# A list schedule with other prices: the same four-layer kernel, planned with instruction durations as costs

## The chip, the cores and the metric

One core of a Trainium2 chip runs the whole program in one launch. The metric is the time of one execution on the device in microseconds. The engines are TensorE (PE; its weight loads are listed as PEld), VectorE (DVE), ScalarE (ACT), GpSimd (POOL) and SyncE (SP), which issues most transfers.

## The reference

A model of four layers on 512 positions of width 1024, in fp32. Each layer is a mixer and a SwiGLU feed-forward part (FFN), each with an RMS norm ahead of it and added to the running sum `h`. The mixers are, in this order, RWKV-7, windowed attention with sinks, a gated spatial unit (SGU) and gated linear attention (GLA).

```python
h = x
for i in range(4):
    hn = rmsnorm(h, norm_mix[i])
    m = [rwkv7_mix, swa_sink_mix, sgu_chunk_mix, gla_mix][i](hn, ...)
    h = h + m
    h = h + swiglu(rmsnorm(h, norm_ffn[i]), ffn_w_in[i], ffn_w_out[i])
return rmsnorm(h, norm_final)

def swiglu(x, w_in, w_out):                  # 1024 -> 2 x 2816 -> 1024
    gate, up = jnp.split(x @ w_in, 2, axis=-1)
    return (jax.nn.silu(gate) * up) @ w_out

# within rwkv7_mix, for 16 heads of 64:
def step(state, inp):
    r_t, d_t, k_t, v_t, kk_t, a_t = inp
    sa = jnp.einsum('bhvk,bhk->bhv', state, kk_t)
    state = (state * d_t[:, :, None, :] - sa[..., None] * (kk_t * a_t)[:, :, None, :]
             + v_t[..., None] * k_t[:, :, None, :])
    return state, jnp.einsum('bhvk,bhk->bhv', state, r_t)
```

## The kernel before, in words

**Products.** A large fp32 product is made of three products in the type fp32r: weights and activations are each split into a high and a low part (`hi` by ScalarE, `lo = raw - hi` by VectorE), and `mm3` adds hi x hi, hi x lo and lo x hi in PSUM. The weights come in tiles of 128 x 1024 (`wraw`, eight buffers), and go through `whi` and `wlo` (four buffers each). The FFN uses a seven-product scheme over quarters (`seven`): each weight quarter is loaded by SP, and combinations of quarters are made by accumulating transfers that POOL issues. For a block of 512 hidden columns a `hidden` pass makes gate and up, and an `out_fast` pass multiplies the result by the output weights and adds into `h`. There are three such output parts in each FFN, fed by two hidden passes each. In an output part of full width there are 14 weight tiles, 16 additions into `h`, 8 combinations of activations and 14 splits of them.

**RWKV.** The scan is worked in chunks of 64 positions. The 16 heads are four groups of four. For each group `rwkv_prepare`, `rwkv_products` and `rwkv_inverse` make decays, scores and an inverse of a triangular matrix (together `ahead(n)`), and `rwkv_chain` goes through eight chunks one after the other: products with the state, a copy by ScalarE (`wu`), 64x64 products with the inverse (`iv`), a copy (`vu`), the state's update by VectorE (`st`), and the outputs. In program order `ahead(n + 1)` stands before the chain of group n. Score blocks are tiles `pa` and `pr`.

**The order.** The kernel isn't emitted as it is written. Every call on an engine is recorded (line 233 of the profile's kernel is the one place that calls the engines, so nearly all instructions bear L233) as an operation with a price: the time for which it occupies its engine, and a latency until its result can be used by a consumer. `Program.run` is a greedy list schedule over all operations. At each step it finds, for every engine, when the operations whose inputs are planned could start; it prefers the lowest in program order among those within `SLACK` (60 ns) of the earliest, in a window of 700 operations, takes the engine whose candidate starts first, and emits it. An operation that touches a tile not held yet also needs a free buffer of its kind, and for PSUM some more conditions. The result is a fixed order of instructions for each engine; on the chip each engine runs its own list in order and waits on semaphores.

**Prices.** `price` gives (occupancy, latency) in ns. `n` is the number of elements a partition, `columns` the number of per-partition scalar operands. An operation's result is ready at occupancy plus latency; the next one on the same engine, if it depends on nothing late, starts after the occupancy. A transposition has 109 ns, an fp32r product 0.4167 ns a column plus 13.5, an fp32 product 1.667 ns a column plus 5.

**Unused products.** The planner also keeps account of the columns that TensorE works on in each stretch of 3413 ns. Where the plan has TensorE waiting and the account is low, `keep_warm` puts in products of the identity with itself whose result nobody reads (line 453, tile `ident`). Their number comes out of the plan. In a stretch that follows one with too little work the plan doubles the cost of products.

Of the kernel before, what the change touches and what calls it, by code (L numbers as in the profile page):

```python
# [189 lines left out]
class Program:  # L190
# [71 lines left out]
    def price(self, eng, what, args, kw):  # L262

        views = [a for a in list(args) + list(kw.values()) if isinstance(a, View)]
        n = max(v.free() for v in views)
        columns = sum(v.free() == 1 and v is not views[0] and n > 1 for v in views)
        if what == "dma_start":
            return (490.0 if eng == "SP" else 1000.0), 2000.0
        if eng == "PE":
            if what == "transpose":  # L270
                return 109.0, 200.0
            m, n = args[1].free(), args[2].free()
            if args[2].dtype == F32R:
                return max(n * 0.4167 + 13.5, m * 0.83), 200.0
            return max(n * 1.667 + 5.0, m * 1.667, 340.0 if n < 16 and m == P else 0.0), 200.0
        if eng == "DVE":
            if what == "memset":
                return n * 1.05, 130.0
            fast = what in ("tensor_copy", "tensor_scalar") and not any(v.buf.psum for v in views)
            return 68.0 + n * (0.52 if fast else 1.042) + 61.0 * columns, 130.0  # L280
        if eng == "ACT":
            return (50.0 if any(v.buf.psum for v in views[1:]) else 92.0) + n * 0.833 + 94.0 * columns, 150.0
        if what == "tensor_copy":
            return 36.0 + n * 3.66, 130.0
        return 37.0 + n * (0.83 if len(views) < 3 else 2.8 if views[0].dims[-1][0] < 32 else 2.32), 130.0

    def run(self):
        ops, n = self.ops, len(self.ops)
# [1492 lines left out]
```

## Time and profile before

| | |
|---|---|
| median of 3 runs | 2627.5 us (2625.31 to 2631.97) |
| the profiled execution | 2641.05 us, its span 2639.3 us |
| mean granted TensorE clock | 0.982 |
| instructions | 34990 |
| busy: PE, PEld, DVE, ACT, POOL | 2554.7, 2083.4, 1853.8, 1331.6, 466.0 us |
| read from HBM | 359.51 MB |

The profile names an instruction by line, engine, operation and tiles (out<-in, buffer numbers left out). "Busy" is the union of the durations on an engine; durations of neighbours can overlap. "Idle before" is the engine's idle time ahead of the instructions of a group, and the arrow names what ended most of it. The windows give busy time in a stretch, the timeline single instructions in order of time, with those of one kind merged (x4 means four).

### The profile page before, as it was taken

How to read it: one execution, taken by the hardware profiler on the slowest of the kernel's cores; microseconds unless marked ns; L12 is line 12 of the kernel's file. 1: busy time of each engine (PE TensorE's matmuls, PEld its weight loads, DVE VectorE, ACT ScalarE, POOL GpSimd, SP SyncE). 2: the span in 40 equal slices, each digit the busy share in tenths (PEclk: the TensorE clock that was granted, in tenths of full speed). 3: DMA queues.
4: the chain of work that ended last, by engine and by line, in shares of the span. 5: the costliest groups of instructions: out<-in, count | busy, mean ns of one | idle time of the engine just before them, and what ended most of it. 6: DMA issues, size and time to landing. Idle time of an engine off the chain costs nothing.

```text
span 2639.3 us, 34990 instructions
## 1 busy us (share of the span) xinstructions
PE 2554.7 (97%) x12974; PEld 2083.4 (79%) x12974; DVE 1853.8 (70%) x2888; ACT 1331.6 (50%) x2208; POOL 466.0 (18%) x492
## 2 busy tenths in 40 slices
PE   8999889999999999999999999999999999999998
PEld 7667767889888775888787888898878777888886
DVE  8675777568787966676868474478777735577868
ACT  3544343356555655655555342365645633555545
POOL 1013333311212234121112000012121000012111
PEclk8989989999999999999999999999999999999999
DMA  3220001148988622499896222379897321389885
GB/s 126 72 68 9 7 7 37 39 126 219 226 215 213 178 84 50 101 223 229 208 227 185 96 96 88 80 176 224 211 228 170 119 96 50 81 221 223 209 209 125
DMA packets 127146, 366.24 MB, mean 139 GB/s; under 512 B 13424, under 2 KB 20976, under 8 KB 126976
## 3 DMA queue, kind: packets, MB, share of 16 engines
q0 software_dynamic: 41472, 138.43, 29.1%
q1 hardware_dynamic: 85504, 225.59, 25.3%
q8 instruction: 102, 1.67, 0.3%
q14 instruction: 68, 0.56, 0.1%
HBM read 359.51 MB, written 2.10 MB: 137 GB/s over the span
## 4 chain that ended last, share of the span: by engine, by line
PE 47%; DMA 5%; issue 5%; DVE 5%; ACT 2%; POOL 0%; SPq 0%; ACTq 0%; POOLq 0%; DVEq 0%
PE ps L233 47%; DMA wraw<-ffn_o_a 2%; DMA wraw<-ffn_w_b 2%; DVE slot L233 2%; DVE wlo L233 1%; ACT whi L233 1%; DVE left L233 1%; DMA wraw<-ffn_w_a 1%; ACT slot L233 1%; POOL wraw L233 0%; DVE h L233 0%; DVE mx L233 0%; DMA wraw<-ffn_o_b 0%; DMA slot<-sg_b_s 0%; DMA slot<-slot 0%
## 5 line engine op out<-in xcount | busy, mean ns | idle before, releaser
L233 PE MATMUL ps<-whi,slot 128*128 128x512 f32 (+1 forms) x5072 | 1548.3, 383 | 14.1 <-DVE slot L233 10.0
L233 PEld LDWEIGHTS ps<-whi,slot 128*128 128x128 f32 x5072 | 942.3, 188 | 190.2 <-issue 22.7
L233 DVE TENSOR_TENSOR wlo<-wraw,whi 128x1024 fp32r<-128x1024 f32 (+2 forms) x628 | 723.1, 1157 | 421.7 <-ACT whi L233 420.5
L233 ACT CAST whi<-wraw 128x1024 fp32r<-128x1024 f32 (+3 forms) x632 | 626.6, 995 | 695.5 <-PE ps L233 528.5
L233 PE MATMUL ps<-wlo,slot 128*128 128x512 f32 (+1 forms) x2536 | 969.3, 382 | 3.7 <-DVE wlo L233 3.6
L233 PEld LDWEIGHTS ps<-wlo,slot 128*128 128x128 f32 x2536 | 476.6, 188 | 87.4 <-DVE wlo L233 7.5
L233 PE MATMUL ps<-slot,whi 128*128 128x512 f32 (+2 forms) x864 | 275.0, 396 | 1.2 <-ACT slot L233 0.9
L233 POOL DMA_DIRECT2D wraw<-ffn_w_a x128 | 109.5, 857 | 502.7 <-DVE wlo L233 363.0
L233 DVE TENSOR_TENSOR slot<-ps,slot 128x512 f32<-128x512 f32 (+2 forms) x287 | 153.3, 566 | 60.4 <-PE ps L233 45.7
L233 PEld LDWEIGHTS ps<-slot,whi 128*128 128x128 f32 (+2 forms) x864 | 156.7, 184 | 48.6 <-issue 9.1
L233 POOL DMA_DIRECT2D wraw<-ffn_w_b x64 | 54.8, 864 | 744.6 <-DMA wraw<-ffn_w_b 505.8
L233 PE MATMUL ps<-slot,wlo 128*128 128x512 f32 (+2 forms) x432 | 169.7, 393 | 0.3 <-DVE wlo L233 0.3
L233 DVE TENSOR_TENSOR slot<-left,slot 128x512 fp32r<-128x512 f32 (+1 forms) x214 | 138.9, 666 | 34.9 <-ACT slot L233 29.1
L233 DVE TENSOR_TENSOR h<-h,ps 128x512 f32<-128x512 f32 x192 | 126.7, 682 | 26.4 <-PE ps L233 25.9
L233 ACT CAST slot<-left 128x512 fp32r<-128x512 f32 (+1 forms) x214 | 124.1, 606 | 31.8 <-PE ps L233 24.7
L233 POOL DMA_DIRECT2D wraw<-ffn_o_a x64 | 54.7, 854 | 278.4 <-DVE wlo L233 162.5
L233 ACT COPY slot<-ps 128x512 f32<-128x512 f32 (+2 forms) x137 | 76.1, 568 | 52.1 <-PE ps L233 51.8
L233 PEld LDWEIGHTS ps<-slot,wlo 128*128 128x128 f32 (+2 forms) x432 | 79.5, 184 | 21.2 <-DVE wlo L233 2.2
L233 PEld LDWEIGHTS ps<-ident,slot 128*128 128x128 f32 x580 | 68.3, 142 | 34.5 <-issue 9.5
L233 PE MATMUL ps<-ident,slot 128*128 128x128 f32 x580 | 89.6, 277 | 3.3 <-POOL slot L233 2.6
L233 ACT COPY left<-ps 128x512 f32<-128x512 f32 x100 | 50.6, 556 | 63.7 <-PE ps L233 63.7
L233 DVE TENSOR_TENSOR slot<-slot 128x512 fp32r<-128x512 f32 (+9 forms) x93 | 61.5, 666 | 18.5 <-ACT slot L233 17.1
(260 smaller groups left out, 2517.3 us busy)
## 6 DMA issues: line engine op xcount, KB each, us to landing
wraw<-ffn_w_a SPq DMA_DIRECT2D x128, 512.0 KB, 6.6
wraw<-ffn_w_a POOLq DMA_DIRECT2D x128, 512.0 KB, 6.0
wraw<-ffn_o_a SPq DMA_DIRECT2D x64, 512.0 KB, 4.8
wraw<-ffn_o_a POOLq DMA_DIRECT2D x64, 512.0 KB, 7.5
wraw<-ffn_w_b SPq DMA_DIRECT2D x64, 384.0 KB, 3.5
wraw<-ffn_w_b POOLq DMA_DIRECT2D x64, 384.0 KB, 6.5
wraw<-ffn_o_b SPq DMA_DIRECT2D x16, 512.0 KB, 5.5
wraw<-ffn_o_b POOLq DMA_DIRECT2D x16, 512.0 KB, 6.1
```

The costliest lines, as they stand in the source:

```text
L233: op = self.add(eng.name, lambda: getattr(eng.target, what)(*map(real, args), **{k: real(a) for k, a in kw.items()}), *self.price(eng.name ...
```

## The change

Only `price` is changed. For VectorE the fixed part goes from 68 to 148 ns and the latency from 130 to 60; a scan has 2.1 ns an element in place of 1.042. For ScalarE the fixed part goes from 50 to 158 (source in PSUM) and from 92 to 195, the latency from 150 to 60. For POOL the fixed part goes from 36 or 37 to 60, the latency from 130 to 60, and the slope of operations on two tensors from 2.8 or 2.32 to 3.25 or 2.5. A product of fp32 type that is 64 in all three sizes has 60 ns in place of 111.7. The operations, their program order and all rules of the planner stay as they are.

```diff
             if args[2].dtype == F32R:
                 return max(n * 0.4167 + 13.5, m * 0.83), 200.0
+            if n == m == views[1].dims[0][0] == 64:
+                return 60.0, 200.0
             return max(n * 1.667 + 5.0, m * 1.667, 340.0 if n < 16 and m == P else 0.0), 200.0
         if eng == "DVE":
             if what == "memset":
-                return n * 1.05, 130.0
+                return n * 1.05, 60.0
             fast = what in ("tensor_copy", "tensor_scalar") and not any(v.buf.psum for v in views)
-            return 68.0 + n * (0.52 if fast else 1.042) + 61.0 * columns, 130.0
+            return 148.0 + n * (0.52 if fast else 2.1 if what == "tensor_tensor_scan" else 1.042) + 61.0 * columns, 60.0
         if eng == "ACT":
-            return (50.0 if any(v.buf.psum for v in views[1:]) else 92.0) + n * 0.833 + 94.0 * columns, 150.0
+            return (158.0 if any(v.buf.psum for v in views[1:]) else 195.0) + n * 0.833 + 94.0 * columns, 60.0
         if what == "tensor_copy":
-            return 36.0 + n * 3.66, 130.0
-        return 37.0 + n * (0.83 if len(views) < 3 else 2.8 if views[0].dims[-1][0] < 32 else 2.32), 130.0
+            return 60.0 + n * 3.66, 60.0
+        return 60.0 + n * (0.83 if len(views) < 3 else 3.25 if views[0].dims[-1][0] < 32 else 2.5), 60.0
```

## The prediction

> **What bounds the kernel now.** I began with the page: busy time by engine, and the slices with the clock that TensorE was granted.
>
> ```profile
> span 2639.3 us, 34990 instructions
> PE 2554.7 (97%) x12974; PEld 2083.4 (79%) x12974; DVE 1853.8 (70%) x2888; ACT 1331.6 (50%) x2208; POOL 466.0 (18%) x492
> PEclk8989989999999999999999999999999999999999
> ```
>
> PE is busy in 97% of the span, so an order can win only what PE stands idle or works at a low clock. The windows, cut at the stages, say where that is (columns: the stretch, its length, then PE, PEld, DVE, ACT, POOL busy us with instructions, granted clock, DMA share, GB/s).
>
> ```profile
> 0.00:198.00 198.00, 185.00 (x776) 136.00 (x777) 149.62 (x252) 94.61 (x147) 19.88 (x17) 0.91 0.26 89
> 198.00:462.00 264.00, 234.76 (x1736) 193.47 (x1735) 192.29 (x369) 113.33 (x239) 97.11 (x94) 0.90 0.05 15
> 462.00:580.00 118.00, 114.50 (x945) 102.55 (x945) 65.54 (x134) 46.79 (x110) 28.05 (x31) 1.00 0.26 83
> 580.00:870.00 290.00, 287.43 (x1371) 242.98 (x1370) 228.23 (x311) 167.30 (x232) 56.01 (x67) 1.00 0.89 212
> 870.00:1066.00 196.00, 187.27 (x862) 131.58 (x860) 143.37 (x263) 111.22 (x289) 66.93 (x57) 0.99 0.37 97
> 1066.00:1386.00 320.00, 316.27 (x1518) 267.74 (x1517) 230.76 (x306) 179.49 (x260) 55.96 (x66) 1.00 0.84 201
> 1690.00:2012.00 322.00, 317.17 (x1517) 267.99 (x1516) 232.02 (x309) 180.98 (x263) 56.95 (x68) 1.00 0.83 197
> 2244.00:2639.00 395.00, 380.35 (x1808) 320.03 (x1806) 287.54 (x414) 214.76 (x328) 61.52 (x72) 0.99 0.75 178
> ```
>
> The first three stretches are the RWKV stage; 580 to 870, 1066 to 1386, 1690 to 2012 and 2244 on are the four FFNs; 870 to 1066 is attention. PE's idle time is length less PE: 13.0, 29.2 and 3.5 us in RWKV (45.7 of the 84.6 us in all, which is 2639.3 - 2554.7), 2.6, 3.7 and 4.8 us in the first three FFNs, 8.7 us in attention, 14.7 us in the last FFN with the tail. The middle of RWKV (198 to 462) also has a clock of 0.90: if the low value is one half, as a mean of 0.90 allows, a fifth of 264 us ran at half speed and cost at most 26 us. So RWKV is where the order counts. In the FFNs PE hardly waits, and the other engines wait for it (waits: engine, tile, releaser, us in all, times, longest):
>
> ```profile
> ACT whi L233 <- PE ps L233: 528.5, 291, 6.8
> DVE wlo L233 <- ACT whi L233: 420.5, 277, 12.2
> ```
>
> **The change, part by part.** No instruction of the algorithm is removed. The diff alters what the planner believes, and through that the order on each engine's queue, and possibly the number of unused products that the planner puts in to hold the clock. So I first ask which prices are nearer to the chip, then what an order made with them does.
>
> *Occupancy of VectorE.* Start, duration and form, in an FFN:
>
> ```profile
> 780.55 1.29 DVE L233 TENSOR_TENSOR h<-h,ps 128x512 f32<-128x512 f32 x2 [0.67 <-PE ps L233]
> 781.75 1.22 DVE L233 TENSOR_TENSOR wlo<-wraw,whi 128x1024 fp32r<-128x1024 f32 x1
> 782.89 1.28 DVE L233 TENSOR_TENSOR h<-h,ps 128x512 f32<-128x512 f32 x2
> 784.09 1.22 DVE L233 TENSOR_TENSOR wlo<-wraw,whi 128x1024 fp32r<-128x1024 f32 x1
> L233 DVE TENSOR_TENSOR h<-h,ps 128x512 f32<-128x512 f32 x192 | 126.7, 682 | 26.4 <-PE ps L233 25.9
> ```
>
> A split lasts 1.22 us, but the next instruction starts 782.89 - 781.75 = 1.14 us after it. Two additions last 0.68 us each and take 1.20 us together, 0.60 each. The old price is 68 + 1024 x 1.042 = 1135 ns and 601 ns: the pitch. The new one, 1215 and 681 ns, is the duration. The engine overlaps the end of one with the start of the next, so the new price books 80 ns too much for each instruction in a run: over 2888 instructions up to 231 us of VectorE time that the chip doesn't spend.
>
> The Trainium skill ("VectorE: DVE Perf Modes", The DRAIN you can't avoid) has it otherwise: the next operation does not start until the pipe is empty, though it adds that one that is not held starts earlier. By that sentence the new price would be the true one and the plan better; these rows, 1.14 us against 1.22 us, speak against it.
>
> *Occupancy of ScalarE and TensorE.*
>
> ```profile
> 341.84 1.27 ACT L233 ACTIVATE ew<-ps,vec 128x512 f32<-128x512 f32 x2
> L233 ACT ACTIVATE ew<-ps,vec 128x512 f32<-128x512 f32 x16 | 10.4, 682 | 0.1
> 335.15 0.68 PE L233 MATMUL ps<-vu,pr 64*64 64x64 f32 x8
> 335.76 0.77 PE L233 MATMUL ps<-ident,qk 128*128 128x128 f32 x5
> L233 PE MATMUL ps<-wu,iv 64*64 64x64 f32 x256 | 22.9, 233 | 1.2 <-ACT wu L233 1.1
> ```
>
> Two activations take 1.27 us at 0.68 each: pitch 0.59. Old price 50 + 426 + 94 = 570, new 678: again pitch against duration, 105 ns too much, over 2208 instructions up to 232 us. For 64x64 products the loops give 4 groups x 8 steps x 4 = 128 with the inverse, and the row has 256 instructions: two for each product. Eight lie (0.68 - 0.233) / 7 = 0.064 us apart, so a product takes 0.128; old price 0.112, new 0.060. The new one is about one instruction's share, half the work. The planner thinks its 256 such products (128 with the inverse, as many with the score blocks) 256 x 0.052 = 13 us cheaper than before.
>
> *Chains.* A wait is priced as occupancy plus latency:
>
> ```profile
> 337.39 0.37 ACT L233 COPY wu<-ps 64x256 f32<-64x256 f32 x1
> 337.81 0.68 PE L233 MATMUL ps<-wu,iv 64*64 64x64 f32 x8 [0.23 <-ACT wu L233]
> 337.14 0.17 DVE L233 TENSOR_TENSOR rs_t<-grs 128x8 f32<-128x8 f32 x1
> 337.34 0.17 DVE L233 SCALAR_TENSOR_TENSOR rs_t<-gvar,rs_t 128x8 f32<-128x8 f32 x1
> L233 DVE TENSOR_TENSOR_SCAN ew<-keep,ew 128x512 f32<-128x512 f32 x8 | 12.1, 1509 | 10.9 <-ACT ew L233 10.9
> ```
>
> From the copy to the product it is 0.42 us; old 50 + 213 + 150 = 413, new 431 ns. Dependent VectorE steps are 0.20 us apart; old 206, new 216. Both are good, the new one 10 to 18 ns a hop on the late side. The scan is the price that gets better: 1.51 us on the chip, old 0.60, new 1.22; 8 x 0.62 = 5 us in RWKV. POOL's prices rise by 7 to 16%; it is busy 18% of the span, and I cost that at nothing where its results are early (its cover is PE's backlog in the FFNs) and take it into RWKV's range.
>
> *What the order does with it, RWKV.* From 198 to 580 us the plan books 503 VectorE instructions x 80 ns = 40 us and 349 on ScalarE x 105 = 37 us that aren't there, and 13 us too little on PE. An engine that seems busy has more instructions ready when it comes free, and the planner then takes the lowest in program order: the preparing of the next group stands ahead of the chain of this one, so the chain's copies queue behind it. Where PE seems to wait, the planner puts in unused products:
>
> ```profile
> L453 PE MATMUL ps<-ident 128*128 128x128 f32 x320 | 58.5, 324 | 1.5 <-POOL ident L233 1.4
> L453 PE MATMUL ps<-ident 128*128 128x128 f32 x220 | 38.7, 307 | 0.1
> ```
>
> The first row is the whole span, the second 198 to 580. 320 instructions are 160 products, some 0.22 us each (the planner's price is 218 ns): 35 us now, 24 of it in these 382 us. The 77 us of booked lateness can't be turned into waits one for one: VectorE and ScalarE have 382 - 258 = 124 and 382 - 160 = 222 us idle there. I take a tenth, +8 us, near the low end of what could show, since PE has other work over most of the stage (from 462 on it is idle for 3.5 of 118 us). Ends: -20 (rival 1's 18 us, and 2 of the scan's 5) and +27 (rival 2).
>
> *The FFNs' output products.*
>
> ```profile
> 800.00:820.00 20.00, 20.00 (x90) 16.55 (x89) 11.64 (x12) 8.58 (x10) 4.26 (x5) 1.00 0.99 200
> 820.00:840.00 20.00, 19.84 (x97) 16.12 (x96) 19.87 (x31) 11.74 (x17) 3.00 (x5) 1.00 0.89 261
> ```
>
> VectorE swings between 11.6 and 19.9 us in 20. An output part has 14 splits, 16 additions to h, 14 splits of activations and 8 combinations: 14 x 1.135 + 38 x 0.601 = 38.7 us by the old price, 42.9 by the new one, beside 168 products at 20 / 90 = 0.222, 37.3 us. The plan believes itself 4.2 us later in each of some 12 such parts (8 of full width). The chip runs at the pitch whatever the plan believes, VectorE has slack in the hidden products before and after (11.64 of 20), and the idle to be lost or won is 2.6 to 4.8 us for a whole FFN. I take 0.3 us a part, +4 us; ends -4 and +12. If the cover of the hidden products goes, it costs the 4.2 us in a part, which the upper end holds for three parts. The transfers' share of 0.89 to 0.99 leaves nothing to gain from an earlier issue; SP's and POOL's issues keep program order unless a buffer frees later in the plan.
>
> *Attention, gating, GLA and the tail.* 8.7 us of idle in attention, 4.4 in gating and GLA together: 0, ends -3 and +5. The tail, within the last FFN's 14.7 us: 0, its instructions being the last in program order by either price.
>
> Sum: 8 + 4 = +12 us. The profiled execution took 2641.05 us (span 2639.3) and would take 2653; the median of the three runs shown is 2627.5, 13.5 below it, so the forecast there is 2639.5, say 2639.
>
> **The rivals.** (1) *Faster: the late prices act as a margin.* Each hop is booked 10 to 18 ns late and each run 80 to 105, so PE is given a product only when its data have surely come; in-order PE stalls less on the chip, where one late producer holds up all behind it. For: RWKV's 29.2 us idle and clock of 0.90, and the scan. Against: in the plan the same margin shows as waits, filled with other work or unused products. At a third of both, 29.2 / 3 + 26 / 3 = 18 us, with nothing for the scan: 2609. The rule on the drain, if it held in most places, gives this time too, by a plan that fits the chip better; I give it 0.03 of this rival's chance.
>
> (2) *Much slower: the chain is starved.* If VectorE and ScalarE take the preparing first everywhere, the chains of two groups run late, with nothing beside them. A step then shows its hops bare: the copy to the product 0.42, the same after the inverse 0.42, the state's update on VectorE
>
> ```profile
> L233 DVE TENSOR_TENSOR st<-ps,st 128x256 f32<-128x256 f32 x28 | 11.8, 421 | 25.5 <-PE ps L233 25.4
> L233 DVE TENSOR_TENSOR st<-st 128x256 f32<-128x256 f32 x24 | 13.1, 545 | 0.4
> ```
>
> 0.42 + 0.545 less 0.08 of overlap: 1.7 us of PE idle, x 16 steps = +27 us, 2654 or 2655. It decides where over half of the last two groups' steps come after the last preparing instruction. Against: only 3.5 us idle after 462 now.
>
> (3) *Nothing moves.* Prices change, yet PE takes the lowest product ready within 60 ns, and PE-bound stages keep their order: within 8 us of 2627.
>
> **How the numbers follow.** About 0.3% (7.9 us) is what a measurement of this kernel tells from no change: 2619.6 to 2635.4. Forecast (2636 to 2648): 0.39. Rival 1: 0.29. Rival 2: 0.13. Rival 3: 0.19. So faster 0.29, same 0.19, slower 0.52. The range takes in rivals 1 and 2 with their ends (-20 to +27 in RWKV, -4 to +12 in the FFNs, on 2627.5): 2604 to 2667; the forecast's own is 2636 to 2648.
>
> **What would show it.** Right: the stretch 198 to 462 longer by some 8 us, with PE's idle time above 29 us or more than 110 of the unused products in RWKV; durations of each form unchanged; FFNs within 3 us each. Rival 1: the RWKV stage shorter, a clock above 0.91 there. Rival 2: PE's idle after the last preparing instruction grows from 3.5 to over 15 us. Wrong altogether: an FFN that changes by over 8 us, or transfers that end later there.

## The result and the profile after

The changed kernel takes 2694.9 us (median of 4 runs, 2689.24 to 2699.32) against 2627.19 us: 67.7 us slower, ratio 1.0254 with a 95% interval of 1.0229 to 1.0279. The profiled execution took 2697.04 us, its span 2695.3. From the page of the changed kernel:

```profile
span 2695.3 us, 35707 instructions
PE 2605.7 (97%) x13312; PEld 2142.5 (79%) x13312; DVE 1877.5 (70%) x2888; ACT 1337.1 (50%) x2206; POOL 467.0 (17%) x492
PEclk9998997999999988999999999999999999999999
L455 PE MATMUL ps<-ident 128*128 128x128 f32 x658 | 111.6, 308 | 2.0 <-POOL ident L233 1.4
L233 DVE TENSOR_TENSOR h<-h,ps 128x512 f32<-128x512 f32 x192 | 128.1, 685 | 33.3 <-PE ps L233 31.2
```

TensorE's share of busy time is unchanged and so is the time of one instruction (685 ns for an addition to `h`, 682 before). New is the number of unused products: 658 instructions are 329 products, 160 before. The other new thing is a dip of the clock in the fifteenth and sixteenth slices, which are the attention stage. The stages, cut at the first instruction that is peculiar to each FFN and at the issue of its last output weights, first of the kernel before (columns as in the prediction):

```profile
0.00:587.10 587.10, 541.36 (x3495) 439.11 (x3496) 414.29 (x775) 261.83 (x509) 145.04 (x141) 0.93 0.17 54
587.10:865.00 277.90, 275.33 (x1308) 231.90 (x1308) 218.02 (x286) 156.37 (x212) 56.01 (x67) 1.00 0.91 217
865.00:1101.00 236.00, 227.27 (x1064) 166.28 (x1064) 163.91 (x301) 136.21 (x342) 67.05 (x58) 0.99 0.36 94
2579.40:2639.30 59.90, 49.10 (x221) 39.76 (x219) 50.79 (x90) 31.96 (x52) 5.12 (x6) 0.94 0.52 117
```

and then of the changed one:

```profile
0.00:606.20 606.20, 555.79 (x3604) 453.33 (x3605) 412.19 (x763) 254.88 (x498) 146.81 (x141) 0.93 0.16 51
606.20:891.50 285.30, 281.09 (x1357) 240.16 (x1356) 226.91 (x297) 163.13 (x222) 55.64 (x67) 1.00 0.90 213
891.50:1146.90 255.40, 243.12 (x1076) 176.58 (x1075) 163.76 (x292) 133.60 (x332) 65.78 (x58) 0.93 0.34 87
2629.10:2695.30 66.20, 51.47 (x238) 41.78 (x236) 51.81 (x90) 32.36 (x52) 5.11 (x6) 0.95 0.47 105
```

RWKV is 19.1 us longer, the first FFN 7.4, attention 19.4, the tail 6.3. The other five stretches together are 3.8 us longer (283.7 for 278.0 in the last FFN, 343.7 for 349.3 in gating). Part of this is work that changed sides of a cut. Counting TensorE's products, without the unused ones, at the pitch of each form, there are some 2414 us of them in both kernels, but 5.7 us fewer stand ahead of the first FFN's mark and 4.5 us fewer in attention, and each FFN has 4.5 to 5.7 us more. With that work put back, RWKV lost 25 us, attention 24, the tail 6 and all FFNs together about 1. On medians RWKV lost some 15 us more than that: in `vector_in_attention` below, which keeps the order of before in that stage, it took 572 us, so the profiled execution of before was a long one in RWKV.

The cover in attention. The windows that follow count only instructions that touch `whi`, that is two in three of the wide products (PE), the casts (ACT) and the splits (DVE) of weights; 20 us each, first before, then after:

```profile
965.00:985.00 20.00, 10.37 (x30) 5.56 (x31) 1.22 (x1) 0.00 (x0) 0.00 (x0) 0.97 0.30 106
1025.00:1045.00 20.00, 7.28 (x21) 3.47 (x20) 1.74 (x1) 0.00 (x0) 0.00 (x0) 1.00 0.07 20
```

```profile
991.00:1011.00 20.00, 0.00 (x0) 0.00 (x0) 0.00 (x0) 0.00 (x0) 0.00 (x0) 0.50 0.24 87
1031.00:1051.00 20.00, 13.38 (x42) 7.67 (x42) 3.38 (x3) 3.16 (x3) 0.00 (x0) 1.00 0.26 66
1051.00:1071.00 20.00, 2.34 (x8) 1.19 (x7) 1.67 (x1) 1.04 (x1) 0.00 (x0) 0.82 0.20 48
```

Before, 18 to 30 of these products stand in every 20 us from 945 to 1065 and fill the gaps between scores, exponentials and transpositions. After, one stretch has none and runs at half the clock, one has 42, the next 8. The wide work is bunched, and the cover is used up where it isn't needed.

Little of attention's loss is idle time of TensorE, which went from 8.7 to 12.3 us. There are also 18 unused products (36 instructions) where there were none:

```profile
L455 PE MATMUL ps<-ident 128*128 128x128 f32 x36 | 7.9, 372 | 0.0
```

The larger part goes with the granted clock, 0.93 for 0.99. If its low value is the 0.50 of the bare stretch, 14% of 255.4 us ran at half speed, which cost at most 18 us, against some 2 us before. This is an estimate from the means of the two windows.

The state update in RWKV. First VectorE's timeline in the kernel before, in the loop that inverts the triangular blocks (`et`, dependent steps), then in the changed one, with the wait of TensorE that it ends:

```profile
342.48 0.15 DVE L233 TENSOR_TENSOR et<-et 128x2 f32<-128x2 f32 x1
342.54 0.42 DVE L233 TENSOR_TENSOR st<-ps,st 128x256 f32<-128x256 f32 x1
342.88 0.14 DVE L233 TENSOR_REDUCE et<-et 128x2 f32<-128x2 f32 x1
342.94 2.04 DVE L233 TENSOR_TENSOR_SCAN ew<-keep,ew 128x512 f32<-128x512 f32 x1
350.85 0.41 DVE L233 TENSOR_TENSOR st<-ps,st 128x256 f32<-128x256 f32 x1
```

```profile
277.86 0.71 PE L233 MATMUL ps<-vu,tok 128*128 128x128 f32 x4 [0.46 <-ACT vu L233]
278.13 0.13 DVE L233 TENSOR_TENSOR et<-et 128x2 f32<-128x2 f32 x1
278.30 0.16 DVE L233 TENSOR_REDUCE et<-et 128x2 f32<-128x2 f32 x1
288.35 0.62 DVE L233 TENSOR_REDUCE et<-et 128x30 f32<-128x450 f32 x1
289.74 0.38 DVE L233 TENSOR_TENSOR st<-ps,st 128x256 f32<-128x256 f32 x1
280.66 4.44 PE L455 MATMUL ps<-ident 128*128 128x128 f32 x32
291.84 1.19 PE L233 MATMUL ps<-st,h 128*128 128x128 f32 x4 [6.74 <-DVE st L233]
```

Before, the loop is laced with other work: the chain's state updates go in between its steps. After, thirty steps run from 278.13 to 288.97 with nothing between them. The product that the state needs (`vu,tok`) is over at 278.57, the update comes at 289.74, and TensorE fills the time with 16 unused products and 6.74 us of idling. The waits of TensorE from 198 us to the first FFN, before and after:

```profile
PE ps L233 <- DVE st L233: 1.2, 1, 1.2
```

```profile
PE ps L233 <- DVE st L233: 12.8, 4, 6.7
```

### The profile page after: what moved, and what is told of

Same layout as the page of the kernel before. It is cut to its first block, busy times and chain, and to the rows that moved or that the text cites. A ratio compares the mean times of both kernels' runs of the same rounds, so it can differ in the third digit from the quotient of the medians.

```text
span 2695.3 us, 35707 instructions
## 1 busy us (share of the span) xinstructions
PE 2605.7 (97%) x13312; PEld 2142.5 (79%) x13312; DVE 1877.5 (70%) x2888; ACT 1337.1 (50%) x2206; POOL 467.0 (17%) x492
## 4 chain that ended last, share of the span: by engine, by line
PE 69%; DVE 3%; DMA 2%; issue 2%; ACT 1%; POOL 0%; SPq 0%; ACTq 0%; DVEq 0%; POOLq 0%
PE ps L233 68%; DVE slot L233 1%; DVE wlo L233 1%; PE ps L455 1%; DMA wraw<-ffn_w_a 1%; DMA wraw<-ffn_o_a 1%; ACT whi L233 1%; ACT slot L233 1%; DVE h L233 1%; DMA wraw<-ffn_w_b 0%; DMA wraw<-ffn_o_b 0%; DMA slot<-slot 0%; POOL wraw L233 0%; DVE mx L233 0%; SPq L233 0%
## 5 line engine op out<-in xcount | busy, mean ns | idle before, releaser
L233 ACT CAST whi<-wraw 128x1024 fp32r<-128x1024 f32 (+2 forms) x632 | 626.2, 993 | 722.9 <-PE ps L233 567.8
L233 PE MATMUL ps<-wlo,slot 128*128 128x512 f32 (+1 forms) x2536 | 969.8, 383 | 10.8 <-DVE wlo L233 10.5
L233 DVE TENSOR_TENSOR slot<-left,slot 128x512 fp32r<-128x512 f32 x214 | 134.9, 651 | 13.1 <-ACT slot L233 9.7
L455 PE MATMUL ps<-ident 128*128 128x128 f32 x658 | 111.6, 308 | 2.0 <-POOL ident L233 1.4
L455 PEld LDWEIGHTS ps<-ident 128*128 128x128 f32 x658 | 99.0, 212 | 12.4 <-issue 3.4
L233 PEld LDWEIGHTS ps<-ident,slot 128*128 128x128 f32 x580 | 70.7, 144 | 34.4 <-POOL slot L233 10.8
```

Of the source, the lines that this page charges most:

```text
L233: op = self.add(eng.name, lambda: getattr(eng.target, what)(*map(real, args), **{k: real(a) for k, a in kw.items()}), *self.price(eng.name ...
L455: self.nc.tensor.target.matmul(self.ps.tile_pool.tile([P, S], F32, name="ps")[:, :P], self.ident.real(), self.ident.real(), start=True, st ...
```

## The experiments

The question for all of them was which price costs, and how. Each is compared with the kernel before on the same chip.

**Which price.** The first four take the prices apart.

`vector_only`: VectorE's lines of the change alone.

> VectorE's new prices alone, all others old. In the plan this has 333 unused products, near the changed kernel's 329 and far from the 160 of before. Theory A (VectorE's over-booked occupancy makes the plan wait and pad): 50 to 75 us slower than before, nearly all of the change's +67. Theory B (several prices together, none decisive): +15 to +35. Theory C (64x64 products priced at half cause it, since the plan thinks TensorE is idle): within 10 us of before.

Measured 2707.96 against 2630.26 us, ratio 1.0311 (1.0284 to 1.0337), +78.

`all_but_vector`: every line of the change but VectorE's.

> The whole change without VectorE's prices (266 unused products in the plan). Theory A: at most +25 us against before. Theory B: +30 to +50. Theory C: +50 or more.

Measured 2674.74, ratio 1.0191 (1.0162 to 1.022), +44: theory B's figure. The parts don't add up (78 + 44 against 68).

`vector_occupancy`:

```diff
-            return 68.0 + n * (0.52 if fast else 1.042) + 61.0 * columns, 130.0
+            return 148.0 + n * (0.52 if fast else 1.042) + 61.0 * columns, 50.0
```

> Only VectorE's fixed occupancy goes from 68 to 148 ns, with the latency cut from 130 to 50 so that a hop to a consumer costs the plan the same 198 ns as before; no price for the scan (330 unused products). Theory A: like VectorE's new prices alone, +50 to +75 us. If the longer hop or the scan were what costs, within 15 us of before.

Measured 2713.11, ratio 1.0341 (1.0311 to 1.0371), +83. Neither the longer hop nor the price of the scan is needed for the loss.

`hops_only`: latency 140 for VectorE, 168 for ScalarE, occupancies as before.

> Occupancies stay at the pitch, and only the latencies rise so that a hop is booked as in the changed kernel (VectorE 130 to 140, ScalarE 150 to 168; 184 unused products). Theory A: within 12 us of before. The margin of the faster rival, by itself: 5 to 20 us faster than before.

Measured 2640.87, ratio 1.0048 (1.0026 to 1.0071), +11. Later release as a margin gained nothing. So theory A held as far as VectorE's prices go: they are enough for the whole loss. It missed that the rest of the change costs 44 us by itself. Whether it is their occupancy these runs don't show: with the sum kept, the latency fell from 130 to 50, below `SLACK`, and the paragraph on the price of a hop, below, comes back to that.

**The unused products.** The plan is left as it is, and only what `keep_warm` emits is changed.

`new_order_no_pad` and `old_order_no_pad`, of the changed kernel and of the one before:

```diff
-            call()
             self.fills += 1
```

> The changed kernel's plan and order exactly, with none of its 329 unused products emitted (the plan still counts them). Theory A1 (the added unused products themselves are what costs, 169 x 0.22 = 37 us): the gap to the kernel of before without its own unused products shrinks from 67 to 30 us or less. Theory A2 (the order on the queues costs, and the products fill idle time): the gap stays at 50 us or more.

> The kernel of before with its order, none of its 160 unused products emitted. Reference for the one above. If the products only fill idle time and hold the clock: slower than before by 5 to 30 us through a lower clock in RWKV. If they cost their time: up to 35 us faster.

Measured 2691.81, ratio 1.0222 (1.0188 to 1.0256), and 2632.97, ratio 1.0018 (1.0002 to 1.0033). The gap between the two orders is 58.8 us without a single unused product: theory A2.

`new_order_pad_rwkv`: the changed kernel, `call()` left out once the first FFN has begun.

> The changed kernel's plan and order, unused products emitted in RWKV alone, those 113 after it left out. Theory A1: 25 us (113 x 0.22) faster than the changed kernel, 2670. Theory A2: within 8 us of it, 2687 to 2703, or slower through the clock in attention.

Measured 2688.98, ratio 1.0222 (1.0191 to 1.0254), 6 us below the changed kernel, or 9 when each is counted from the kernel before that was measured beside it. That is at the edge of what theory A2 allowed, and far from theory A1's 25.

`old_order_pad_twice`: `call()` twice.

> The kernel of before with each of its 160 unused products emitted twice, the plan unchanged. Theory A1: 25 to 35 us slower than before (160 x 0.22 = 35). Theory A2: within 10 us of before, since they lie where TensorE waits anyway.

Measured 2635.88, ratio 1.0026 (1.001 to 1.0041): 160 more products for 6 us. They lie where TensorE waits anyway. Twice as many of them in the changed kernel is a sign of what the plan believes, and makes at most 9 of the 68 us (67.7 less 58.8). The loss is in the order.

**Where.** VectorE over-booked as in `vector_occupancy`, but only for operations recorded in some stages; here attention.

```diff
+            if self.stage == ('mix', 1):
+                return 148.0 + n * (0.52 if fast else 1.042) + 61.0 * columns, 50.0
             return 68.0 + n * (0.52 if fast else 1.042) + 61.0 * columns, 130.0
```

`vector_in_rwkv`:

> VectorE over-booked (148 and 50 in place of 68 and 130) only for operations recorded in RWKV, the pitch elsewhere. Theory L (the cost is made where chains and wide products have to be interleaved, each stage for itself): +25 to +45 us, all of it before the first FFN. Theory S (the cost comes from the order over stage borders, so no stage alone has it): under +12.

Measured 2686.52, ratio 1.0218 (1.0197 to 1.0239), +60, more than expected.

`vector_in_attention`:

> VectorE over-booked only for operations recorded in the attention stage. Theory L: +12 to +30 us, between the first FFN's last weights and the start of the second FFN, with stretches of 20 us there that hold hardly a wide product. Theory S: under +8.

Measured 2641.41, ratio 1.0046 (1.0031 to 1.0061), +15.

`vector_elsewhere`:

> VectorE over-booked in all stages but RWKV and attention: the FFNs, gating, GLA, the end (249 unused products in the plan, though RWKV's prices are old). Theory L: within 12 us of before, most of it in the tail. If the FFNs' output parts, where VectorE is fullest, were what costs: +20 us or more, 1.5 or more in each of 12 parts.

Measured 2644.09, ratio 1.0057 (1.0038 to 1.0076), +17, above what theory L allowed. RWKV and attention are both over theory S's bounds. Each has its loss at its place. The first two windows are RWKV and attention of `vector_in_rwkv`, the others those of `vector_in_attention`:

```profile
0.00:638.50 638.50, 580.98 (x3653) 472.10 (x3654) 418.84 (x775) 267.24 (x512) 148.54 (x141) 0.90 0.16 49
917.40:1153.40 236.00, 227.23 (x1064) 166.32 (x1064) 163.74 (x301) 136.13 (x342) 67.04 (x58) 0.99 0.36 95
```

```profile
0.00:572.10 572.10, 524.72 (x3495) 425.67 (x3496) 413.88 (x775) 261.69 (x509) 145.40 (x141) 0.96 0.17 55
850.20:1103.20 253.00, 240.75 (x1083) 175.07 (x1082) 170.30 (x303) 137.54 (x342) 61.85 (x58) 0.94 0.34 88
```

Attention takes 236.0 us with the old price (as in the kernel before) and 253 with the new one, and RWKV 638.5 against 572.1. The second pair also shows that an RWKV of the same instructions can take 572.1 us at a clock of 0.96 or 587.1 at 0.93. In `vector_elsewhere` an FFN takes 282 to 291 us, of which 4.5 to 4.8 are work that stood outside its marks before. With that taken off, the last FFN lost 8.5 us (291.3 for 278.0) and the tail 5.0 (64.9 for 59.9), most of the 17; the other three FFNs lost 1.5 together.

**Over-booking or any other price.** `vector_under_booked`: 28 and 170 in place of 68 and 130.

> The other sign: VectorE's fixed occupancy 28 ns in place of 68, latency 170, so that a hop costs the plan the same (193 unused products). Theory O (over-booking is what hurts, since it piles up ready operations): within 12 us of before, or faster. Theory D (any price off the pitch hurts): 20 us slower or more.

Measured 2696.83, ratio 1.0261 (1.0244 to 1.0278), +70. That ended my theory that over-booking as such costs. Two theories were left: the loss follows the error of a price, or the order of before is a good draw that nearly any change loses.

`price_2ns_off`: 66 and 132 in place of 68 and 130.

> VectorE's fixed occupancy 66 ns in place of 68, latency 132, all else as before. Theory E (the loss follows the error of the price): within 5 us of before. Theory N (the order of before is one good draw among many, and any other is worse): +10 us or more; the plan has 224 unused products in place of 160, though the price moved by 2 ns.

Measured 2655.43 against 2626.44, ratio 1.0111 (1.0095 to 1.0126): 29 us from 2 ns, as theory N had it and theory E not. The loss is in RWKV, 601.8 us in its profile.

`price_corrected`: the scan at 2.4 ns an element, a 64x64 product at 128 ns.

> Two prices brought to what the profile of before shows: the scan at 2.4 ns an element (1.30 us for 512; 0.60 before) and a 64x64 product at 128 ns (112 before); all else as before, 176 unused products. Theory E: 0 to 10 us faster than before. Theory N: 5 us slower or more.

Measured 2634.32, ratio 1.0043 (1.0025 to 1.0061): 8 us slower with two prices nearer to the chip, again theory N.

`product_64_only`: the change's 60 ns alone.

> The changed kernel's 60 ns for a 64x64 product alone (half of what it takes), all else as before, 188 unused products. Theory E: the planner errs by 256 x 0.068 = 17 us in RWKV alone, +5 to +17 us there. Theory N: +5 to +40 us, not bound to RWKV.

Measured 2638.69, ratio 1.0049 (1.0037 to 1.0062), +12; both theories had that, and it doesn't tell them apart.

`window_500`: the look-ahead of the planner 500 operations in place of 700.

> No price changed: the planner looks 500 operations ahead in place of 700 (150 unused products). Theory E says nothing of it, within 8 us of before. Theory N: another draw, 5 us slower or more, unless the stage orders stay as they are; if it is faster by over 8 us it beats both kernels.

Measured 2626.15, ratio 0.9996 (0.9981 to 1.0012). The 5 us that theory N asked for didn't come in the whole. In its profile RWKV took 560.5 us, attention 247.4: one won, the other lost.

**A version that is faster than both.** `window_500_rwkv` takes the shorter look-ahead in RWKV alone, `window_500_2ns` the same with 66 and 132 there.

```diff
+            first = head < self.border
+            self.WINDOW, self.SLACK = (500, 60.0) if first else (700, 60.0)
```

> Prices as before; look-ahead of 500 operations in RWKV, 700 after it (150 unused products). From the traces of window_500: RWKV 12 us shorter than in before's shortest profile (560.5 against 572), attention as before (236 against 247 there): 8 to 14 us faster than before.

> The same with VectorE's fixed occupancy 66 and latency 132 in RWKV (147 unused products). If 2 ns in the price cost by themselves: 20 us or more above the kernel beside it. Theory N (the order found by chance is what counts, and here the plan has no jump): within 6 us of it.

`window_500_rwkv` took 2610.69 against 2625.92 us, ratio 0.9938 (0.9917 to 0.996): 15 us faster than before, and so some 83 faster than the changed kernel. Its RWKV and attention:

```profile
0.00:557.60 557.60, 518.03 (x3469) 420.55 (x3470) 409.39 (x775) 261.68 (x509) 145.41 (x141) 0.96 0.18 56
836.90:1072.70 235.80, 226.03 (x1065) 165.23 (x1064) 163.77 (x303) 136.27 (x342) 67.09 (x58) 1.00 0.36 95
```

`window_500_2ns` took 2625.34, ratio 0.9991 (0.9971 to 1.0011), 15 us above its neighbour: neither within 6 us nor 20 above. Two nanoseconds cost half of what they cost at a look-ahead of 700, and that decides for neither theory.

## Why the prediction was right or wrong

**Right.** The change is slower; that had a chance of 0.52, and most of the loss came from a term put at 0 and from one put too small, so the sign is in part luck. The prices of before are the pitch and the new ones the duration, and the durations stayed. The faster rival has no support (`hops_only` +11). Rival 3, that the order hardly moves, is out. Two readings were off by little: the windows give 4.1 us of idle time for gating and GLA, not 4.4, and the scan's 1.51 us is the mean of eight durations from 1.21 to 2.17 us.

**The FFNs' output parts (+4).** All FFNs together lost about 1 us in the profile, although the plan believed VectorE 4.2 us late in each part; by length alone they grew by 7.4, 3.3, 4.3 and 5.7 us, beyond my mark of 3, but that is the work that came over to them. With VectorE's price alone, in all stages but RWKV and attention, they lost 10 us, 8.5 of it in the last. So 4 us lies between two orders made with much the same prices there, and neither bears out the way in which I got it, by a share of the booked lateness.

**Attention (0, ends -3 and +5): this step failed.** It measured +24. I looked at its 8.7 us of idle time and took that for the room that an order has. What was at stake was the cover that kept the idle time at 8.7 and the clock at 0.99: the wide products between the scores. Even after the loss the idle time is only 12.3 us; the clock is 0.93 (0.94 in `vector_in_attention`). A stage in which TensorE is busy only since two kinds of work are laced together has as much to lose as one of them can leave bare, and that isn't read from its idle time.

**RWKV (+8, ends -20 and +27): mis-sized.** It lost 25 us in the two profiles and some 40 against the usual length of that stage before. Rival 2 named something that the trace shows, preparing that goes ahead of the chain on VectorE, but not its place: I looked for it after 462 us, and it sits in the middle, in the inverse's loop. How much of the loss it makes isn't settled (next paragraph). My mark for it, over 15 us of idle after the last preparing instruction, didn't come: from the end of the last loop to the first FFN TensorE idles for 7.8 us, and 7.4 before. Of the forecast's own marks, more than 29 us of idle time from 198 to 462 didn't come (27.7), and more than 110 unused products did (145 from 198 to 580). In all of RWKV TensorE's idle time went from 45.7 to 50.4 us only, and the unused products from 145 to 216: they fill such idle time, so that idle time was the wrong mark.

**What the price of a hop hid.** I added occupancy and latency (198 and 208 ns), found the sum right, and passed on. The planner uses the two apart. While a dependent step waits out its latency, VectorE is free in the plan, and another operation goes in between only if it can start over `SLACK`, 60 ns, earlier. The change sets the latency to 60, so nothing ever can. The orders bear it out. In the kernels with VectorE's latency at 50 or 60 in RWKV (the changed one and the two with its order, `vector_only`, `vector_occupancy`, `vector_in_rwkv`) all four loops run bare in 10.8 to 11.1 us. In the kernel before they hold 2, 13, 13 and 10 other instructions and take 12.9 to 25.3 us, and in the others with a latency above 60 they hold 2 to 27. The planner's own order, worked out without the chip, changes over at one nanosecond: at a latency of 61 the loops are laced, at 60 bare, with the occupancy at 68 and at 148 alike. RWKV takes 606 to 639 us in the kernels with bare loops and 558 to 603 in all others. A stage can lose without them, too: in `all_but_vector` the loops hold 2 to 9 other instructions, and RWKV takes 594 us (572 to 587 in the order of before) and attention 250 (236). What share of the loss that has on the chip isn't settled: no kernel was run on the chip with the occupancy at 148 and the latency above 60, and `window_500_rwkv`, the fastest, also has long waits for the state:

```profile
PE ps L233 <- DVE st L233: 11.2, 8, 4.0
```

So these waits alone don't make a slow RWKV. What is shown is that the order costs (58.8 us without any unused product), that RWKV and attention have the most of it, and which rule makes the loops bare. How much of the rest is the bunching of wide work, as in attention, stays open.

**The tail (0): +6.3 us.** I had it that its instructions are the last in program order by either price. The same 215 of the model's products start there in both kernels; that there are 238 instructions for 221 comes from the unused products, 10 for 2. But TensorE idles for 14.7 us among them, and 10.8 before. This part follows the price: in the six kernels with VectorE's occupancy at 148 in the last stages the tail takes 64.9 to 66.5 us, in the other fourteen 59.9 to 61.2.

**The range.** It ended at 2667, from the named mechanisms' prices in two stages; not even attention's own +5 was in it. It left out what the small changes showed: the order of before is a good draw. 2 ns on one price cost 29 us, two corrected prices 8, one halved price 12, and a shorter look-ahead nothing. For a greedy plan that depends on ties, the spread over small changes belongs in the range, whatever the change means. That alone may not make up the 68 us. `hops_only`, `price_2ns_off`, `price_corrected`, `product_64_only` and `window_500` cost 0 to 29 us; the five kernels with a whole engine's prices far off in all stages (the changed one, `vector_only`, `all_but_vector`, `vector_occupancy`, `vector_under_booked`) cost 44 to 83. Five of each suggest that the size of the change counts too, and don't show it.

## What to carry to other kernels

Where an order comes out of a greedy list schedule, look at how the rules use each number: here a latency equal to the planner's tolerance meant that a serial loop never yields the engine. A stage's idle time bounds what an order can win, not what it can lose; for that, look at how much of its busy time is work of another kind laced in as cover. Before a price is called better, try a price that is a nanosecond or two off: if that moves the time as much, the order is a draw, and looking at other draws (here a shorter look-ahead in one stage, 15 us) can pay more than truer prices (here a loss of 8).

## What the runs showed that I had not expected

All 160 unused products can be left out for 2.9 us, or doubled for 5.8, though they were there to hold the clock: without them RWKV's profile has a clock of 0.94 and 574.9 us, with them 0.93 and 587.1 or 0.96 and 572.1, by the same order. So the granted clock of that stage differed by 0.03, and its length by 15 us, between two executions of one order.
